# One value product of 256 columns per group, a sum moved to the branch's load, and one ring for the small tiles

## The chip, the cores and the metric

The kernel runs on one core of a Trainium2 chip. The metric is the device time of one execution in microseconds. A core has five engines that run side by side and wait for one another by semaphores: TensorE (PE, matrix products; its weight loads are listed apart as PEld), VectorE (DVE), ScalarE (ACT), GpSimd (POOL) and SyncE (SP), which here only issues DMAs. PE writes its results to PSUM, eight banks of 512 fp32 columns; the other engines read them there and put them into SBUF.

## The reference

One layer of an encoder over 1024 tokens of 1024 channels, in fp32:

```python
h = h + 0.5 * swiglu(rms_norm(h, ffn1_norm), ...)
u = rms_norm(h, mix_norm)
z = u @ w_in
q, k, v, s_in, gates = jnp.split(z, splits, axis=-1)
y_attn = neighbourhood_attention(q, k, v, na_rpb) @ w_attn_out
y_ssm = s5_branch(s_in, ...) @ w_ssm_out
g_attn, g_ssm = jnp.split(jax.nn.sigmoid(gates), 2, axis=-1)
h = h + (g_attn * y_attn + g_ssm * y_ssm) @ w_out
h = h + 0.5 * swiglu(rms_norm(h, ffn2_norm), ...)
h = h + (p @ w_ple_proj) * sigmoid(rms_norm(h, ple_norm) @ w_ple_gate)
return rms_norm(h, final_norm)
```

The attention has 8 heads of 64 channels. The tokens are a grid of 16 rows by 64 columns; each token attends to a window of 8 rows by 16 columns around it, clamped inside the grid. In the inner loop: `sc = q.k * scale + bias`, `pr = softmax(sc)`, `out = sum(pr * v)`. The other branch, S5, is a complex state-space scan over the tokens in both directions, followed by a GLU.

## The kernel before

**Two parts of every number.** The kernel gives PE its large products in fp32r, a rounded form. So that the result stays close to fp32, each operand is split into a high part, a rounded copy made on ACT, and a low part, the difference, made on DVE (`split`, L150-152). A full product is three: high x high, high x low, low x high (`mm3`, L180-184).

**Stages.** First FFN (0 to some 700 us), then the mixer (the input projections, attention, scan and GLU, to 1172 us), the two branch projections and the merge by gates, the output projection, the second FFN and the last embedding. In the mixer two streams are interleaved on PE. The main stream makes the projections: q and k of a pair of heads (`qk_proj`), and gate tiles (`gate_tile`, whose result `gs` goes to the scratch g_d in HBM). The side stream is the generator `mixer_side` (L1280 on). Each time that the main stream has issued the three products of one block it calls `tick()`, and the generator goes on after as many ticks as it asked for (4 in the first 48 units of attention, 3 after that). PE runs in exactly the order of the program; the order on DVE, ACT, POOL and SP is chosen by a planner that follows the program's priorities and a simulated time.

**Attention.** A unit is a head `hd`, a half of the rows `rb` (8 rows) and a column block `cb` of 16 columns: 8 x 2 x 4 = 64 units of 128 query tokens. A unit looks at 12 rows by 24 or 32 columns of keys, so it has 288 or 384 scores per query. Its work is spread over several steps of the loop:

- step j: `attn_scores` of unit j. Two products give the scores `s`, DVE adds the bias table, ACT makes the exponential and scales by the reciprocal of the sum; the result is `sm`.
- step j+3: `attn_turn`. Three transposes on PE into a PSUM bank `pt`; ACT copies the high part to `pth`, DVE makes the low part `ptl` (L1220, L1221).
- step j+5: `attn_values`. The weights are the values, held in `vhl` as [keys, 4 groups, 2 parts, 64 channels]. For each of three groups of keys there are two products: the values' high and low parts together (128 columns of weights) on `pth`, and the high part alone (64 columns of weights) on `ptl` (L1229, L1231). Each streams the unit's 128 queries into its 128 columns of the bank `O`, which serves four units, one (hd, rb). Channels stand on partitions 0 to 63; partitions 64 to 127 get the part of the values' low half. After the fourth unit ACT copies the upper half to `ol`, DVE adds it to the lower half, in token order, into `ot` (L1235, L1236), and ACT's queue stores `ot` to the scratch `o_d` [512, 1024].

In the loop (L1312 on) step j calls `attn_scores`, then `attn_turn`, then `attn_values`, then, for rb = 1, `load_v` of the next head (4 loads on SP, a cast on ACT, a subtraction on DVE), then two steps of the scan, which runs on POOL. From j = 48 on, each step also has `ssm_out` of one of 16 pairs of state groups: it loads two `emi` tiles on SP, copies states `xs`, and three steps later makes six products each for two groups into the bank `yo`; the result `ys` is stored to y_d. After that come the GLU's weights (`wgs`), its inputs (`yg`, split to `yh`, `yl`) and its eight products with `sg`, stored to y2_d.

**The branch's load.** `load_br(t, 0)` (L1394) loads `o_d` back for half t of the tokens, two loads of [128, 1024] into tiles `br`, and splits them; the products `br` use them at the end of the mixer.

**Rings.** A tile comes from a ring of equal slots and waits until one is free. In the mixer: the large ring `x` of 56 slots of [128, 512] (all of `tx` and `thid`: 32 slots hold u, its two parts, to the end of the mixer; `vhl`, `sm`, `pth`, `ptl`, `emi` and the GLU's split tiles share the rest); the ring of small tiles `tmp`, 4 slots (`gs`, `vf`, `row`, `ys`, `ot`, `ol`, `sg`, `wgs` and others); `st`, 3 slots of [128, 1024] (loads); `w`, 12 slots (weights and states). PSUM banks are a ring of eight.

Of the kernel before, what the change touches and what calls it, by code (L numbers as in the profile page):

```python
# [16 lines left out]
P = 128  # L17
SEQ = 1024
# [20 lines left out]
def encoder_block(ctx, tc, I, out):  # L39
# [50 lines left out]
    def dtile(name, shape):  # L90
        return dr.tile(list(shape), F32, name=name)
# [62 lines left out]
    def ksl(k):  # L154
        return slice(k * P, (k + 1) * P)
# [1057 lines left out]
    def attn_turn(cb, sm):  # L1213
        kp = 4 * KNC[cb]
        tp = bank("pt")
        for g in range(3):
            T.transpose(tp[0:kp, ksl(g)], sm[:, g * kp:(g + 1) * kp], ident)
# [6 lines left out]
    def attn_values(hd, rb, cb, O, ph, pl):  # L1224
        kp = 4 * KNC[cb]
        hl = vld[hd, cb]
        for g in range(3):

            T.matmul(O[:, ksl(cb)], lhsT=hl[0:kp, rb + g].rearrange("p h d -> p (h d)"), rhs=ph[0:kp, ksl(g)], start=(g == 0), stop=False,  # L1229
                     skip_group_check=True)  # L1230
            T.matmul(O[0:64, ksl(cb)], lhsT=hl[0:kp, rb + g, 0], rhs=pl[0:kp, ksl(g)], start=False, stop=(g == 2),  # L1231
                     skip_group_check=True)
        if cb == 3:
            ot, ol = tmp("ot"), tmp("ol")
            A.copy(ol[0:64], O[64:128])  # L1235
            V.tensor_tensor(ot[0:64].rearrange("p (r b c) -> p b r c", r=8, b=4),  # L1236
                            O[0:64].rearrange("p (b r c) -> p b r c", b=4, r=8),
                            ol[0:64].rearrange("p (b r c) -> p b r c", b=4, r=8), ALU.add)
# [41 lines left out]
    def mixer_side():  # L1280
# [31 lines left out]
        for j in range(n + 6):  # L1312
            if j < n:
                hd, rb, cb = units[j]
                while hd not in qkv:
                    yield 1
                if cb == 0 and j > 0:
                    make_tabs(hd, rb)
                sms[j] = attn_scores(hd, rb, cb)
            if 0 <= j - 3 < n:  # L1320
                pts[j - 3] = attn_turn(units[j - 3][2], sms.pop(j - 3))
            if 0 <= j - 5 < n:
                hd, rb, cb = units[j - 5]
                if cb == 0:
                    O[hd, rb] = bank("O")
                attn_values(hd, rb, cb, O[hd, rb], *pts.pop(j - 5))
                if rb == 1 and hd + 1 < NH:
                    load_v(hd + 1, cb)
            scan_steps(2)
            if j >= SO:  # L1330
                p = j - SO
# [62 lines left out]
    def load_br(t, b):  # L1394

        res = []
        if b == 0:
            for k in range(0, 4, 2):
                st = tst("br")
                nc.sync.dma_start(st.rearrange("p (k c) -> p k c", k=2),  # L1400
                                  o_d[k * P:(k + 2) * P, hsl(t)].rearrange("(k p) c -> p k c", p=P))
# [402 lines left out]
```

## Time and profile before

| | |
|---|---|
| median of 3 runs | 2105.99 us (2104.8 to 2106.98) |
| the profiled execution, its own time | 2106.49 us |
| its span | 2104.7 us |
| PE, PEld, DVE, ACT, POOL busy over the span | 99%, 81%, 67%, 48%, 19% |
| mean granted PE clock | 0.996 |
| value products on `pth` (L1229), on `ptl` (L1231) | 192 and 192, from 853 to 1109 us |
| sums of O (L1236) | 16, from 866.5 to 1113.6 us |
| PE idle in the whole span | 27.5 us |

How to read it: the time runs from launch to end on the device, the span from the first to the last instruction that the profiler shows. Durations of products overlap, because products are pipelined and their ends modelled; what a product costs is the distance from its start to the next start. "PEclk" is the part of full speed that PE's clock was granted. A row of a wait names the instruction that waited, and in brackets how long and for what.

### The profile page before, as it was taken

To read this page: it belongs to the slowest core of one execution; us is meant where nothing else is said; L and a number is where in the kernel's file an instruction comes from. 1 tells how busy PE (TensorE), PEld (TensorE's weight loads), DVE (VectorE), ACT (ScalarE), POOL (GpSimd) and SP (SyncE) were. 2 spreads that over 40 slices of the span, in tenths; PEclk is the share of its full clock that TensorE was granted. 3 is DMA by queue.
4 is the path that set the end of the run, shared out by engine and by line. 5 is a ranking of instruction groups with operands and counts; after the bars stand their busy time and mean duration, and the time that the engine had idled before them with its cause. 6 is when DMAs were issued, how large, how long until landed. Compare 5 with 4: busy or idle time off the path is not lost.

```text
span 2104.7 us, 28050 instructions
## 1 busy us (share of the span) xinstructions
PE 2077.2 (99%) x9660; PEld 1707.4 (81%) x9660; DVE 1414.2 (67%) x2420; ACT 1000.3 (48%) x1832; POOL 401.7 (19%) x636
## 2 busy tenths in 40 slices
PE   8999999999999999999999999899999999999997
PEld 3788888888888888888888888788888888888886
DVE  7897776667967334777653658896566665786855
ACT  6434333434445333667674635543333334445544
POOL 0047555541000006888100011000000000000000
PEclk9999999999999999999999999999999999999999
DMA  3434444475533552233477754143323338533302
GB/s 133 143 118 154 126 134 126 140 269 165 185 119 107 167 177 68 64 102 97 120 202 263 254 171 91 56 159 111 110 85 126 90 112 296 158 109 92 119 21 81
DMA packets 197455, 285.19 MB, mean 136 GB/s; under 512 B 41536, under 2 KB 80576, under 8 KB 197312
## 3 DMA queue, kind: packets, MB, share of 16 engines
q1 hardware_dynamic: 180160, 258.22, 38.9%
q10 hardware_dynamic: 14848, 20.98, 2.9%
q0 software_dynamic: 2304, 4.20, 1.3%
q8 instruction: 76, 1.25, 0.3%
q14 instruction: 67, 0.55, 0.1%
HBM read 201.01 MB, written 82.31 MB: 135 GB/s over the span
## 4 chain that ended last, share of the span: by engine, by line
PE 93%; DVE 4%; ACT 1%; DMA 1%; issue 1%; SPq 0%; DVEq 0%; ACTq 0%
PE dx L182 4%; PE dx L183 4%; PE dx L184 4%; PE ux L182 3%; PE ux L184 3%; PE ux L183 3%; PE gx L182 3%; PE gx L183 3%; PE gx L184 3%; PE gt L182 3%; PE gt L183 3%; PE gt L184 3%; PE dy L183 2%; PE dy L182 2%; PE dy L184 2%; PE uy L182 2%
## 5 line engine op out<-in xcount | busy, mean ns | idle before, releaser
L151 ACT CAST wh<-hbuf 128x512 fp32r<-128x512 f32 x280 | 172.9, 622 | 392.3 <-PE gx L183 84.0
L152 DVE TENSOR_TENSOR wl<-hbuf,wh 128x512 fp32r<-128x512 f32 x280 | 210.4, 754 | 125.2 <-ACT wh L151 123.0
L151 ACT CAST wh<-wblk 128x512 fp32r<-128x512 f32 x190 | 117.8, 622 | 182.5 <-PE dx L183 78.5
L182 PE MATMUL dx<-ah,wh 128*128 128x512 f32 x416 | 164.0, 394 | 3.9 <-DVE hbuf L1548 3.6
L152 DVE TENSOR_TENSOR wl<-wblk,wh 128x512 fp32r<-128x512 f32 x190 | 130.3, 688 | 53.4 <-ACT wh L151 48.0
L184 PE MATMUL dx<-ah,wl 128*128 128x512 f32 x416 | 162.3, 390 | 0.0
L183 PE MATMUL dx<-al,wh 128*128 128x512 f32 x416 | 162.3, 390 | 0.0
L152 DVE TENSOR_TENSOR al<-araw,ah 128x512 fp32r<-128x512 f32 x154 | 106.0, 692 | 53.7 <-PE dx L183 21.1
L1086 POOL TENSOR_TENSOR sc<-X,rho 128x128 f32<-128x128 f32 x128 | 77.9, 609 | 327.1 <-ACT X L1069 317.1
L182 PE MATMUL gx<-xh,wh 128*128 128x512 f32 x320 | 125.0, 391 | 1.3 <-DVE c L571 1.2
L182 PE MATMUL ux<-xh,wh 128*128 128x512 f32 x320 | 125.1, 391 | 0.3 <-DVE c L571 0.3
L184 PE MATMUL gx<-xh,wl 128*128 128x512 f32 x320 | 124.5, 389 | 0.0
L184 PE MATMUL ux<-xh,wl 128*128 128x512 f32 x320 | 124.5, 389 | 0.0
L183 PE MATMUL ux<-xl,wh 128*128 128x512 f32 x320 | 124.5, 389 | 0.0
L183 PE MATMUL gx<-xl,wh 128*128 128x512 f32 x320 | 124.5, 389 | 0.0
L151 ACT CAST ah<-araw 128x512 fp32r<-128x512 f32 x154 | 95.0, 619 | 47.5 <-PE dx L183 12.7
L182 PE MATMUL gt<-xh,wh 128*128 128x512 f32 x256 | 103.0, 402 | 0.0
L183 PE MATMUL gt<-xl,wh 128*128 128x512 f32 x256 | 99.9, 390 | 0.0
L184 PE MATMUL gt<-xh,wl 128*128 128x512 f32 x256 | 99.8, 390 | 0.0
L182 PEld LDWEIGHTS dx<-ah,wh 128*128 128x128 f32 x416 | 78.4, 188 | 21.8 <-issue 4.7
L414 DVE TENSOR_TENSOR hbuf<-hbuf 128x512 f32<-128x512 f32 x120 | 91.2, 761 | 2.1
L183 PEld LDWEIGHTS dx<-al,wh 128*128 128x128 f32 x416 | 78.5, 189 | 16.8 <-issue 0.7
(379 smaller groups left out, 5592.0 us busy)
## 6 DMA issues: line engine op xcount, KB each, us to landing
araw<-a_d SPq DMA_DIRECT2D x154, 256.0 KB
a_d<-c SPq DMA_DIRECT2D x148, 256.0 KB
wblk<-in_wd SPq DMA_DIRECT2D x88, 256.0 KB
hbuf<-in_wg SPq DMA_DIRECT2D x40, 512.0 KB
hbuf<-in_wu SPq DMA_DIRECT2D x40, 512.0 KB
wst<-in_win SPq DMA_DIRECT2D x26, 512.0 KB
hbuf<-in_xT SPq DMA_DIRECT2D x32, 256.0 KB
h_d<-hbuf ACTq DMA_DIRECT2D x32, 256.0 KB
```

The source lines that it names most:

```text
L151: A.copy(hi, src)
L152: return eng.tensor_tensor(lo, src, hi.bitcast(F32), ALU.subtract)
L182: T.matmul(o, lhsT=wh, rhs=xh, start=first, stop=False, skip_group_check=more)
L183: T.matmul(o, lhsT=wh, rhs=xl, start=False, stop=False, skip_group_check=more)
L184: T.matmul(o, lhsT=wl, rhs=xh, start=False, stop=last, skip_group_check=more)
L414: V.tensor_tensor(b11, (b12, b22, None, None, b21)[i - 2], b11, ALU.subtract)
L1086: G.tensor_tensor(sc, both, rho4, ALU.mult)
```

## The change

- `attn_turn` writes both parts of the turned weights into one tile `pb` of [keys, 3 groups, 2 parts, 128 queries], from a ring of its own with 2 slots. ACT's cast and DVE's subtraction stay, with the same sizes.
- `attn_values` makes one product per group in place of two: 128 columns of weights (both parts of the values) on 256 columns (both parts of the attention weights). A unit fills 256 columns of a bank, so a bank `O` serves two units. After every second unit ACT copies two parts (each 64 partitions x 256 columns) to the tile `O["t"]`, and DVE adds the third to the lower one. The fourth quarter, low part on low part, is not read. The upper and lower halves are no longer added here: after the fourth unit both go to `o_d`, which gets a leading dimension of 2, in one store of 128 partitions.
- `load_br(t, 0)` loads both halves (two `br` tiles per two row blocks) and DVE adds them, [128, 1024] each, before the split.
- The order in a step of the loop becomes scores, values (with `load_v`), turn.
- In the mixer the small tiles come from the large ring of 56 slots; their own ring of 4 is gone.

```diff
-    o_d = dtile("o_d", [512, SEQ])
+    o_d = dtile("o_d", [2, 512, SEQ])
...
-    cur.update(st=(ap_, "st", 3), w=(ap_, "w", 12), tmp=(ap_, "tmp", 4))
+    cur.update(st=(ap_, "st", 3), w=(ap_, "w", 12), tmp=(sb, "x", NX))
...
-        ph = thid("pth", [P, 384])
-        pl = thid("ptl", [P, 384])
-        A.copy(ph[0:kp], tp[0:kp, 0:384])
-        V.tensor_tensor(pl[0:kp], tp[0:kp, 0:384], ph[0:kp].bitcast(F32), ALU.subtract)
-        return ph, pl
+        pb = ap_.tile([P, 3, 2, P], F32R, tag="ptb", bufs=2, name="ptb")
+        src = tp[0:kp, 0:384].rearrange("p (g q) -> p g q", g=3)
+        A.copy(pb[0:kp, :, 0], src)
+        V.tensor_tensor(pb[0:kp, :, 1], src, pb[0:kp, :, 0].bitcast(F32), ALU.subtract)
+        return pb
...
+        o = O["o"][:, (cb % 2) * 256:(cb % 2) * 256 + 256]
         for g in range(3):
-            T.matmul(O[:, ksl(cb)], lhsT=hl[0:kp, rb + g].rearrange("p h d -> p (h d)"), rhs=ph[0:kp, ksl(g)], start=(g == 0), stop=False,
+            T.matmul(o, lhsT=hl[0:kp, rb + g].rearrange("p h d -> p (h d)"), rhs=pb[0:kp, g].rearrange("p h q -> p (h q)"), start=(g == 0), stop=(g == 2),
                      skip_group_check=True)
-            T.matmul(O[0:64, ksl(cb)], lhsT=hl[0:kp, rb + g, 0], rhs=pl[0:kp, ksl(g)], start=False, stop=(g == 2),
-                     skip_group_check=True)
+        if cb % 2 == 0:
+            return
+        if cb == 1:
+            O["t"] = tmp("ot")
+        ov = O["t"].rearrange("p (r b c) -> p b r c", r=8, b=4)[:, cb - 1:cb + 1]
+        src = O["o"].rearrange("p (b h r c) -> p h b r c", b=2, h=2, r=8)
+        A.copy(ov[64:128], src[64:128, 0])
+        A.copy(ov[0:64], src[0:64, 0])
+        V.tensor_tensor(ov[0:64], src[0:64, 1], ov[0:64], ALU.add)
         if cb == 3:
-            ot, ol = tmp("ot"), tmp("ol")
-            A.copy(ol[0:64], O[64:128])
-            V.tensor_tensor(ot[0:64].rearrange("p (r b c) -> p b r c", r=8, b=4),
-                            O[0:64].rearrange("p (b r c) -> p b r c", b=4, r=8),
-                            ol[0:64].rearrange("p (b r c) -> p b r c", b=4, r=8), ALU.add)
-            nc.scalar.dma_start(o_d[hd * 64:(hd + 1) * 64, hsl(rb)], ot[0:64])
+            nc.scalar.dma_start(o_d[:, hd * 64:(hd + 1) * 64, hsl(rb)], O["t"])
...
+            if 0 <= j - 5 < n:
+                hd, rb, cb = units[j - 5]
+                if cb % 2 == 0:
+                    O.setdefault((hd, rb), {})["o"] = bank("O")
+                attn_values(hd, rb, cb, O[hd, rb], pts.pop(j - 5))
+                if rb == 1 and hd + 1 < NH:
+                    load_v(hd + 1, cb)
             if 0 <= j - 3 < n:
                 pts[j - 3] = attn_turn(units[j - 3][2], sms.pop(j - 3))
-            if 0 <= j - 5 < n:
...
-                st = tst("br")
-                nc.sync.dma_start(st.rearrange("p (k c) -> p k c", k=2),
-                                  o_d[k * P:(k + 2) * P, hsl(t)].rearrange("(k p) c -> p k c", p=P))
+                st = [tst("br") for _ in range(2)]
+                for w in range(2):
+                    nc.sync.dma_start(st[w].rearrange("p (k c) -> p k c", k=2),
+                                      o_d[w, k * P:(k + 2) * P, hsl(t)].rearrange("(k p) c -> p k c", p=P))
+                V.tensor_tensor(st[0], st[0], st[1], ALU.add)
                 for i in range(2):
                     hi, lo = tx("bh"), tx("bl")
-                    split(hi, lo, st[:, hsl(i)])
+                    split(hi, lo, st[0][:, hsl(i)])
```

More of the change, by code (lines that the diff above doesn't have):

```diff
@@ L1217, in attn_turn, with attn_values @@
             T.transpose(tp[0:kp, ksl(g)], sm[:, g * kp:(g + 1) * kp], ident)
[L1218 to L1224 removed]
+        pb = ap_.tile([P, 3, 2, P], F32R, tag="ptb", bufs=2, name="ptb")
[3 more added lines that the diff above has]
+        return pb
+    def attn_values(hd, rb, cb, O, pb):
         kp = 4 * KNC[cb]
         hl = vld[hd, cb]
+        o = O["o"][:, (cb % 2) * 256:(cb % 2) * 256 + 256]
         for g in range(3):
[L1229 removed]
+            T.matmul(o, lhsT=hl[0:kp, rb + g].rearrange("p h d -> p (h d)"), rhs=pb[0:kp, g].rearrange("p h q -> p (h q)"), start=(g == 0), stop=(g == 2),
                      skip_group_check=True)
[L1231 to L1239 removed]
+        if cb % 2 == 0:
[7 more added lines that the diff above has]
+        V.tensor_tensor(ov[0:64], src[0:64, 1], ov[0:64], ALU.add)
+        if cb == 3:
+            nc.scalar.dma_start(o_d[:, hd * 64:(hd + 1) * 64, hsl(rb)], O["t"])
     ydr = y_d.rearrange("g (t o) c -> g o t c", o=16)
@@ L1319, in mixer_side @@
                 sms[j] = attn_scores(hd, rb, cb)
+            if 0 <= j - 5 < n:
[5 more added lines that the diff above has]
+                    load_v(hd + 1, cb)
             if 0 <= j - 3 < n:
                 pts[j - 3] = attn_turn(units[j - 3][2], sms.pop(j - 3))
-            if 0 <= j - 5 < n:
[L1323 to L1328, printed above, removed]
             scan_steps(2)
```

## The prediction

> **What bounds the kernel now.** I read the page first (busy shares and the chain that ended last), then the table of stretches, then TensorE's timeline through single attention units, then the waits.
>
> ```profile
> span 2104.7 us, 28050 instructions
> PE 2077.2 (99%) x9660; PEld 1707.4 (81%) x9660; DVE 1414.2 (67%) x2420; ACT 1000.3 (48%) x1832; POOL 401.7 (19%) x636
> PE 93%; DVE 4%; ACT 1%; DMA 1%; issue 1%; SPq 0%; DVEq 0%; ACTq 0%
> ```
>
> TensorE (PE) is busy 99% of the span and carries 93% of the chain. So a change counts for what it takes from PE's own stream, and for the waits that it puts into it or takes out. The next table is for the stretch that the change touches: length, busy time of PE, of weight loads (PEld), DVE, ACT and POOL, granted clock, DMA share.
>
> ```profile
> 850.00:900.00 50.00, 50.00 (x298) 43.46 (x296) 36.91 (x85) 34.32 (x76) 42.98 (x90) 1.00 0.25 74
> 1000.00:1050.00 50.00, 47.95 (x300) 42.66 (x299) 32.43 (x82) 33.80 (x78) 10.20 (x23) 0.97 0.41 118
> ```
>
> In the attention PE has no gap; DVE and ACT are at some 70%, so neither is a bound there. One stretch has a gap of 2 us and a clock under 1.
>
> **The value products.** One attention unit on PE's timeline, from its scores to the projection that follows (start, duration as modelled):
>
> ```profile
> 926.26 0.29 PE L1201 MATMUL s<-kh,qs 128*128 128x288 f32 x1
> 926.39 0.30 PE L1202 MATMUL s<-kl,qs 128*128 128x288 f32 x1
> 926.52 0.49 PE L1217 MATMUL pt<-ident,sm 128*128 128x128 f32 x3
> 926.77 0.30 PE L1229 MATMUL O<-pth,vhl 96*128 96x128 f32 x1
> ...
> 927.25 0.23 PE L1231 MATMUL O<-ptl,vhl 96*64 96x128 f32 x1
> 927.32 0.44 PE L182 MATMUL q<-xh,wh 128*128 128x512 f32 x1
> 927.60 0.40 PE L183 MATMUL q<-xl,wh 128*128 128x512 f32 x1
> ...
> 929.87 0.39 PE L184 MATMUL q<-xh,wl 128*128 128x512 f32 x1
> 930.10 0.34 PE L1201 MATMUL s<-kh,qs 128*128 128x384 f32 x1
> ...
> 931.54 0.39 PE L183 MATMUL q<-xl,wh 128*128 128x512 f32 x1
> ```
>
> Products overlap, so starts are compared, not durations. From 927.60 to 929.87 lie ten steps of 512 columns: 0.227 us each. The unit with 288 score columns runs from 926.26 to 927.60, 1.34 us, of which 0.227 is the first q product: 1.11 us for the attention part. The one with 384 columns: 931.54 - 930.10 - 0.227 = 1.21 us. What sets the pace of the six value products is seen in the weight loads of another unit:
>
> ```profile
> 922.90 0.19 PEld L1229 LDWEIGHTS O<-pth,vhl 128*128 128x128 f32 x1
> 923.01 0.14 PEld L1231 LDWEIGHTS O<-ptl,vhl 128*64 128x64 f32 x1
> 923.08 0.19 PEld L1229 LDWEIGHTS O<-pth,vhl 128*128 128x128 f32 x1
> ```
>
> They run without a gap: 0.11 us for 128 columns, 0.06 for 64, 0.17-0.18 a pair, so three pairs are 0.51-0.54 us and the next product still waits for its weights (0.28 from 927.32 to 927.60 where 0.227 is usual). The Trainium skill (TensorE: Matmul & The Clock Gate, "LDWEIGHTS (loading the stationary operand)") gives columns over 1.2 GHz, as an estimate 0.107 and 0.053 us; the rows agree within 0.02. The change keeps three loads of 128 columns and streams 256 columns behind each. The price of that is in the last stage, 24 steps between these two rows:
>
> ```profile
> 2084.74 0.28 PE L182 MATMUL pg<-xh,whh 128*128 128x256 f32 x1
> 2087.62 0.28 PE L182 MATMUL pp<-pph,whh 128*128 128x256 f32 x1
> ```
>
> 2.88 / 24 = 0.12 us for 256 columns with a new load each. A unit in the new order is then 0.13 + 0.13 (scores) + 3 x 0.12 (values) + 3 x 0.11 (transposes, a load of 128 columns each) = 0.95 us, against 1.11. With 384 columns: 0.18 + 0.18 + 0.36 + 0.33 = 1.05 against 1.21. That is 0.16 us in both, times 64 units = 10.2 us off PE. Bounds: 0.13 if the load behind the transposes still shows by 0.03 (8.3 us), 0.20 if the whole of 0.54 - 0.36 and a bit of the late projection comes back (12.8 us).
>
> **The place where PE waited.** The small tiles leave a ring of 4 for the ring of 56. What the 4 cost is in this place:
>
> ```profile
> 1033.39 4.06 DMA y_d<-ys
> 1037.53 0.56 DVE L1180 TENSOR_TENSOR row<-bt,rowm 128x384 f32<-128x384 f32 x1 [2.66 <-DMA y_d<-ys]
> 1040.87 0.68 DVE L1236 TENSOR_TENSOR ot<-O,ol 64x512 f32<-64x512 f32 x1
> 1034.73 0.23 PE L1231 MATMUL O<-ptl,vhl 96*64 96x128 f32 x1
> 1036.41 0.40 PE L183 MATMUL gt<-xl,wh 128*128 128x512 f32 x1
> 1039.33 0.22 PE L1231 MATMUL O<-ptl,vhl 96*64 96x128 f32 x1
> 1041.60 0.79 PE L1111 MATMUL yo<-emi 128*128 128x128 f32 x2 [2.05 <-DVE ot L1236]
> 1044.75 0.46 PE L183 MATMUL gt<-xl,wh 128*128 128x512 f32 x1
> ```
>
> `row` (L1180) and `ys` are both small tiles. DVE stood 2.66 us for a slot that a store of `ys` still held; `ot` behind it came late, and PE stood 2.05 us for it. After that PE ran slower for a while. From the last value product to the second projection product it took 5.42 us here and 1.68 in the unit before, so 3.74 us were lost. With 24 slots beside the 32 that hold u, `row` need not wait for that store: I take 3.7 us off. Bounds: 0 if another wait takes its place, 4.3 if the 0.54 us wait quoted under the rivals goes too.
>
> **Evacuation.**
>
> ```profile
> L1235 ACT COPY ol<-O 64x512 f32<-64x512 f32 x15 | 8.8, 584 | 1.8 <-DMA y_d<-ys 1.4
> L1115 ACT COPY ys<-yo 128x256 f32<-128x256 f32 x16 | 5.9, 367 | 2.9 <-PE yo L1113 1.7 <-DMA y_d<-ys 0.9
> L1236 DVE TENSOR_TENSOR ot<-O,ol 64x512 f32<-64x512 f32 x15 | 10.2, 680 | 4.2 <-ACT ol L1235 4.1
> L1165 DVE TENSOR_TENSOR vhl<-vf,vhl 128x256 fp32r<-128x256 f32 x14 | 6.9, 491 | 5.1 <-ACT vhl L1164 5.1
> L152 DVE TENSOR_TENSOR wl<-wst,wh 128x1024 fp32r<-128x1024 f32 x14 | 18.4, 1316 | 2.4 <-PE s L1201 1.6 <-PE yo L1113 0.7
> ```
>
> Per head and half ACT makes four copies of 256 columns out of PSUM in place of one of 512 at 0.58: by the nearest row 0.37 each, together +0.9 us (at most 0.58 each, +1.75). DVE makes two sums of about 0.49 in place of one of 0.68: +0.3. Over the four units, some 15.5 us, ACT goes from about 10.6 busy to 11.6 of 14.9 us, 78%; DVE stays below that. Nothing of this is on PE's path as long as an O bank comes back before PE runs round the eight; O is now held for two units rather than four. If the cover is gone, the 16 x 0.9 = 14 us that ACT gains in work (28 at most) are what it could cost. The splits of the weights cost the same as before; their pair has two slots, and values now run ahead of the transposes, so the slot is free when the next pair is written. `load_v` moves with the values: four loads on SP, a cast on ACT and a subtraction on DVE per block now stand ahead of the transposes' cast and subtraction, whose reader is two units off; no queue entry of SP or POOL lies between the old place and the new. Stores of O stay 16 issues on ACT's queue, of 256 KB for 128.
>
> **The branch's load.** Eight loads in place of four go through a ring of three, and four sums of 128x1024 are added on DVE, 1.32 us each by L152. When are they due?
>
> ```profile
> 1146.36 2.67 SPq L1400 DMA_DIRECT2D br<-o_d  x2
> 1143.05 2.56 ACT L151 CAST bh<-br 128x512 fp32r<-128x512 f32 x4
> L182 PE MATMUL br<-bh,wh x32: 389/389/389, 1172.2 to 1193.3; 128*128 128x512 f32 x32
> 1173.56 1.29 DVE L152 TENSOR_TENSOR bl<-br,bh 128x512 fp32r<-128x512 f32 x2 [1.07 <-ACT bh L151]
> ```
>
> The first half is split from 1143 and used from 1172: 29 us of cover. The second is split until 1174.9 and due 24 products later, at 1172.2 + 24 x 0.227 = 1177.6: 2.7 us of cover. Its loads were issued from 1146 on, 27 us before the split of 1173.56, so the sums fit ahead of the splits; if they don't, up to 2 x 1.32 us of sum plus a late fourth load show, less the 2.7. On SP a fourth load that waits for a slot holds the g_d stores and h_d loads behind it; in a ring of 56 the stores' tiles are not missed at once. I take 0; bounds 0 and +4.
>
> **Sum.** The profiled execution took 2106.49 us (span 2104.7, 1.8 around it), 0.5 above the median of 2105.99. 2106.5 - 10.2 - 3.7 = 2092.6; I add 1.1 for two waits of the 0.54 kind in the crowded last units: 2093.7, in terms of the median about 2093.
>
> **Rivals.** *Given back in part.* The big ring is crowded in units 48 to 63.
>
> ```profile
> 1090.27 0.46 PE L1111 MATMUL yo<-emi 128*128 128x128 f32 x2 [0.54 <-DMA emi<-u_d]
> 1086.95 3.19 DMA emi<-u_d
> SPq L1096 <- PE yo L1113: 1.0, 3, 0.4
> ```
>
> SP already waits there for slots that state products (yo) set free, and PE once for a load that came late. Counting tiles from the code: 32 of u, 4 to 8 of values, 4 of softmax, 8 of emi are up to 52 of 56; the pairs (6) leave, and some 5 to 9 small tiles come. If the 3.7 us wait merely moves, or a few of 1 us appear, the time is 2097 to 2101.
>
> *Slower: the full ring starves the state products.* If small tiles take the slots early and each of the 16 pairs' emi loads is issued only when a slot frees, PE waits at every pair, for between 0.54 (the one seen) and 3.19 us (the whole landing). At 1.5 us that is +24: 2117. It decides from 14 / 16 = 0.87 us per pair. For it: the count above. Against: in most pairs emi is issued several microseconds ahead, and total room (60 slots of both rings, then 56 and the pairs outside) is not less.
>
> *No gain in the products.* If columns streamed set the pace, 6 x 128 and 3 x 256 cost the same 0.36 us (3 x 0.12), and only the wait's 3.7 us remain: 2102. The gapless loads and the 0.51 us of the six speak against it. The Trainium skill (TensorE: Matmul & The Clock Gate, "Back-to-back issue gap") has a gap formula for isolated products, by which I estimate 0.335 us for the six and 0.328 for the three; this trace disagrees with it for the six (0.51). The same section says that in a stream of loads and products both set the spacing, and with that the rows agree.
>
> *It does not do what it says.* DVE, ACT and SP are ordered by a planner; a new order can put waits of a few microseconds anywhere behind the attention and leave nothing measurable.
>
> **Chances.** A measurement can tell about 0.2% (4.2 us) from no change: 2101.8 to 2110.2. Forecast (2087 to 2097) 0.60; given back in part 0.24; no gain in the products 0.02; planner 0.05; starved ring 0.09. So faster 0.84, same 0.07, slower 0.09. Low end: 2106 - 12.8 - 4.3 = 2089, and 3 us for an order that happens to be better; high end 2104, which leaves out the starved ring and part of the planner's case.
>
> **What the profile after would show.** Right: O products 3 per unit, 256 columns, 0.12 us apart; the part from scores to projection 0.95 and 1.05 us; no DVE wait of `row` for a `ys` store and clock 1.00 in all stretches of the attention; ACT near 78% there. Wrong if: starts of O are over 0.15 us apart; yo waits for emi at many pairs; ACT waits for slots of `gs` or `sg` around the GLU, where 32 of u, 8 of its weights and 16 of its inputs fill all 56; or the first products of branch 0's second half wait for a sum.

## The result, and the profile after

The changed kernel takes 2179.15 us (median of 4 runs, 2171.54 to 2182.62) against 2106.48 for the kernel before on the same chip: a ratio of 1.034 (95% interval 1.0328 to 1.0353). The forecast was 2093. The profiled execution took 2177.57 us, 71.1 more than the one of before; the spans differ by 71.0. The page of the changed kernel, busy times and chain:

```profile
span 2175.7 us, 27724 instructions
PE 2098.3 (96%) x9468; PEld 1711.9 (79%) x9468; DVE 1417.7 (65%) x2440; ACT 1011.0 (46%) x1882; POOL 400.9 (18%) x636
PE 78%; DMA 9%; DVE 6%; ACT 4%; SPq 2%; issue 1%; DVEq 0%; ACTq 0%
```

PE is still busy nearly always, but its share of the chain fell from 93 to 78%, and transfers hold 9% of it. No engine got much more work (ACT 11 us, DVE 4). PE now waits. The two stretches shown of before, in the changed kernel (length, then PE, PEld, DVE, ACT, POOL busy, granted clock, DMA share, GB/s):

```profile
850.00:900.00 50.00, 50.00 (x261) 43.03 (x260) 33.07 (x85) 33.93 (x83) 42.79 (x93) 1.00 0.23 69
1000.00:1050.00 50.00, 43.96 (x221) 37.60 (x222) 34.86 (x90) 36.74 (x89) 17.90 (x39) 0.93 0.27 85
```

At 850 the attention runs without a gap; at 1000 PE stands 6 of 50 us and its clock falls. One unit on PE's timeline, as the change makes it:

```profile
888.61 0.29 PE L1201 MATMUL s<-kh,qs 128*128 128x288 f32 x1
888.74 0.30 PE L1202 MATMUL s<-kl,qs 128*128 128x288 f32 x1
888.87 0.52 PE L1231 MATMUL O<-ptb,vhl 96*128 96x256 f32 x3
889.23 0.49 PE L1217 MATMUL pt<-ident,sm 128*128 128x128 f32 x3
889.48 0.48 PE L182 MATMUL k<-xh,wh 128*128 128x512 f32 x1
889.79 0.39 PE L183 MATMUL k<-xl,wh 128*128 128x512 f32 x1
```

Three value products start 0.36 us ahead of the transposes, so 0.12 each, and the attention part is 889.79 - 888.61 - 0.227 = 0.95 us. That is the forecast to the hundredth, so the loss lies elsewhere. The waits of PE between 680 and 1340 us (who waited for whom: us in total, times, longest):

```profile
PE br L182 <- ACT bh L151: 13.3, 3, 6.0
PE pt L1217 <- ACT gs L1362: 10.5, 4, 5.1
PE yo L1111 <- DVE ptb L1221: 4.6, 4, 1.2
```

They name ACT and DVE, which are busy for 66 to 73% of the two stretches above: those wait in their turn. The chain through 905 to 960 us (start, us) and ACT's waits for the loads of v, of the changed kernel and then of the kernel before:

```profile
910.03 7.52 DMA vf<-v_d
926.71 8.19 DMA vf<-v_d
945.27 8.74 DMA o_d<-ot
956.29 2.29 DMA vf<-v_d
```

```profile
  DMA vf<-v_d: 64.2, 22
```

```profile
  DMA vf<-v_d: 13.3, 10
```

A load of v that is free takes 2.3 us, others take 7.5 to 8.6, and on the whole chain of the attention the store of O itself takes 8.7 to 11.1. The DMA view of the changed kernel from 1014 to 1024 us, with one such store in it (busy share of the 16 DMA engines in 40 slices, GB/s, and the share of ACT's queue):

```profile
DMA  3221211222123012111111111111111111111000
GB/s 69 57 59 28 68 38 28 47 56 55 38 57 46 0 53 50 53 56 57 41 57 49 52 43 55 46 46 47 54 46 47 46 54 47 45 35 30 2 0 0
q10 hardware_dynamic: 130, 0.26, 7.9%
```

While hardly anything but the 256 KB of this store is under way, the busy share stays at 1 tenth and the rate at 41 to 57 GB/s. A stretch in the store that ends the chain's row of 945.27, with the share in hundredths (last columns: clock, DMA share, GB/s):

```profile
951.00:953.00 2.00, 2.00 (x14) 1.79 (x14) 1.74 (x4) 1.66 (x4) 1.64 (x5) 1.00 0.13 48
```

0.13 is two engines of sixteen. The store's target has two planes, and its outermost dimension is 2. The Trainium skill (DMA: Bandwidth & Descriptors, "Why a DMA increments its semaphore by 16 and not by 1") states that a DMA runs on the largest number of engines up to 16 that divides the outermost dimension of both sides; the trace agrees, with 2.

To see where the 71 us lie I cut each profile at the first start of a group of PE's products and at their last (us; "state products" from the first yo to the last, "branch" from the first br of L182 to the last br). The stretches are those of the profiled execution, the time is the median of the runs:

| kernel | time | sin to scores | scores to first yo | state products | branch | rest |
|---|---|---|---|---|---|---|
| before | 2106.5 | 151.1 | 193.8 | 73.4 | 86.8 | 1599.6 |
| after | 2179.2 | 162.1 | 205.9 | 99.5 | 107.5 | 1600.7 |
| e1 two stores | 2138.2 | 162.2 | 187.7 | 78.9 | 107.3 | 1600.5 |
| e3 only the ring | 2141.9 | 161.1 | 196.4 | 79.9 | 102.9 | 1600.3 |
| e5 only the order | 2110.8 | 152.1 | 194.1 | 78.3 | 86.8 | 1599.9 |
| e9 before, rings 11/3 | 2105.0 | 151.6 | 193.8 | 73.1 | 86.8 | 1597.8 |
| e7 two stores, rings 11/3 | 2112.3 | 152.1 | 187.5 | 76.2 | 94.6 | 1599.9 |
| e12 one store, rings 11/3 | 2185.1 | 152.4 | 225.9 | 100.7 | 96.4 | 1609.3 |
| e8 sums at evacuation, 11/3 | 2105.6 | 151.8 | 187.5 | 75.9 | 86.8 | 1599.0 |
| e14 the same, 10/5 | 2093.2 | 152.6 | 187.5 | 68.4 | 86.8 | 1596.0 |
| e16 two stores, 10/5 | 2101.1 | 151.4 | 187.5 | 71.0 | 87.1 | 1600.7 |
| e17 before, 10/5 | 2104.3 | 151.5 | 193.8 | 70.1 | 86.8 | 1601.7 |
| e22 e14 with 8 stores into planes | 2108.5 | 151.2 | 188.9 | 81.8 | 86.8 | 1596.4 |
| e23 e14 with 8 flat stores | 2094.9 | 151.8 | 187.6 | 69.2 | 86.8 | 1596.6 |
| e24 one flat store, 10/5 | 2103.5 | 151.2 | 187.5 | 67.5 | 96.0 | 1600.4 |
| e25 e14 in the large ring | 2127.7 | 160.7 | 187.5 | 72.7 | 104.4 | 1602.5 |

"11/3" means 11 weight tiles and 3 small tiles in rings of their own. The rest is the stretch before sin, the pieces between, and some 845 us behind the branch. From kernel to kernel it moves by some 3 us either way (in e12 it is 9.7 more than before, nearly all between the last state product and the GLU), so a single difference of 3 us isn't read as an effect.

### The profile page after: what moved, and what is told of

Read it like the earlier page. It is cut to its first block, busy times and chain, and to the rows that moved or that the text cites. A ratio compares the mean times of both kernels' runs of the same rounds, so it can differ in the third digit from the quotient of the medians.

```text
span 2175.7 us, 27724 instructions
## 1 busy us (share of the span) xinstructions
PE 2098.3 (96%) x9468; PEld 1711.9 (79%) x9468; DVE 1417.7 (65%) x2440; ACT 1011.0 (46%) x1882; POOL 400.9 (18%) x636
## 4 chain that ended last, share of the span: by engine, by line
PE 78%; DMA 9%; DVE 6%; ACT 4%; SPq 2%; issue 1%; DVEq 0%; ACTq 0%
PE dx L182 4%; PE dx L183 4%; PE dx L184 4%; PE gx L182 3%; PE ux L182 3%; PE gx L184 3%; PE ux L184 3%; PE ux L183 3%; PE gx L183 3%; DMA o_d<-ot 3%; DMA vf<-v_d 2%; PE dy L183 2%; PE dy L182 2%; PE dy L184 2%; PE gy L182 2%; PE uy L182 2%
## 5 line engine op out<-in xcount | busy, mean ns | idle before, releaser
L182 PE MATMUL dx<-ah,wh 128*128 128x512 f32 x416 | 164.3, 395 | 1.4 <-DVE hbuf L1555 1.1
L182 PE MATMUL gx<-xh,wh 128*128 128x512 f32 x320 | 125.0, 390 | 1.2 <-DVE c L571 1.2
L182 PE MATMUL ux<-xh,wh 128*128 128x512 f32 x320 | 125.0, 390 | 0.0
L182 PE MATMUL gt<-xh,wh 128*128 128x512 f32 x256 | 104.8, 410 | 2.8 <-ACT ys L1115 2.8
L182 PEld LDWEIGHTS dx<-ah,wh 128*128 128x128 f32 x416 | 78.4, 189 | 19.5 <-DVE hbuf L1555 1.9
```

The source lines that it names most:

```text
L182: T.matmul(o, lhsT=wh, rhs=xh, start=first, stop=False, skip_group_check=more)
```

## The experiments

**The change with one part undone, and two parts alone.** Two stores of 64 partitions in place of one of 128:

```diff
-            nc.scalar.dma_start(o_d[:, hd * 64:(hd + 1) * 64, hsl(rb)], O["t"])
+            for w in range(2):
+                nc.scalar.dma_start(o_d[w, hd * 64:(hd + 1) * 64, hsl(rb)], O["t"][w * 64:(w + 1) * 64])
```

> The changed kernel with each 128-partition store of O made as two stores of 64 partitions each; nothing else. Theory S (slow store): the store to the two halves of o_d runs on two of the sixteen DMA engines (DMA share 0.13, 46 to 48 GB/s, 8 to 9 us), and the slots and value loads behind it starve PE; with two stores of the old form it lands in under 4 us and most of the 46 us lost in the attention units come back: 2125 to 2140. Theory R (ring): the small tiles in the ring of 56 starve the planner's order by themselves: 2165 to 2182, PE still waits in the units.

Measured: 2138.16 us, ratio 1.015 (1.0133 to 1.0168). That is within theory S. The same bytes in twice as many issues are 41 us faster than the change. The stretch from the scores to the first state product falls from 205.9 to 187.7 us, below the 193.8 of before. 32 us of loss remain, nearly all from sin to the scores and in the branch.

The kernel before with the small tiles in the large ring, and nothing else of the change:

```diff
-    cur.update(st=(ap_, "st", 3), w=(ap_, "w", 12), tmp=(ap_, "tmp", 4))
+    cur.update(st=(ap_, "st", 3), w=(ap_, "w", 12), tmp=(sb, "x", NX))
```

> The kernel before with only the small tiles put into the large ring. Theory S: only the losses outside the units appear, 10 us before the first scores and some around the GLU: 2112 to 2135, no new loss per unit. Theory R: the units lose as well, 2150 or more. My forecast of a gain from the removed wait of row for ys: 2102.

Measured: 2141.86 us, ratio 1.0175 (1.016 to 1.019). That is above theory S, whose range ended at 2135, and below theory R. The shared ring alone costs 36 us: 10.0 from sin to the scores, 16.1 in the branch, and 9.1 in the attention, where theory S expected no new loss. What it does in the first of these is seen on DVE, where the blocks of the projections' input are normalised (xn, a small tile) and split. Kernel before:

```profile
698.96 2.74 DVE L254 SCALAR_TENSOR_TENSOR xn<-hbuf,gains,rs 128x512 f32<-128x512 f32 x4
702.75 2.49 DVE L152 TENSOR_TENSOR xl<-xn,xh 128x512 fp32r<-128x512 f32 x4
```

Changed kernel:

```profile
707.84 0.69 DVE L152 TENSOR_TENSOR xl<-xn,xh 128x512 fp32r<-128x512 f32 x1 [0.69 <-ACT xh L151]
708.44 0.75 DVE L254 SCALAR_TENSOR_TENSOR xn<-hbuf,gains,rs 128x512 f32<-128x512 f32 x1
709.88 0.69 DVE L152 TENSOR_TENSOR xl<-xn,xh 128x512 fp32r<-128x512 f32 x1 [0.69 <-ACT xh L151]
```

Before, four xn are made in a row, and ACT casts one while DVE makes the next. After, the next xn starts only when the xl of the last is through, DVE stands 0.69 us for ACT in each block, and a block takes 709.88 - 707.84 = 2.04 us in place of (2.74 + 2.49) / 4 = 1.3. This run (e3) has the same pattern, with xl at 707.97 and 710.01. PE's own waits for these blocks are only 1.8 us in e3, but its granted clock falls to 0.50 between 715 and 720 us, and from 710 to 720 us it starts 20 products where the kernel before starts 48. In effect the small tiles have one slot there, not four; as I read it, u and the prefetches fill the large ring, and a small tile gets a place only as its predecessor leaves. That it is the ring is shown by this run, whose only edit it is; how the ring comes to have one slot for them is not shown.

The kernel before with the values ahead of the transposes, and nothing else of the change:

```diff
-            if 0 <= j - 3 < n:
-                pts[j - 3] = attn_turn(units[j - 3][2], sms.pop(j - 3))
             if 0 <= j - 5 < n:
                 hd, rb, cb = units[j - 5]
...
                 if rb == 1 and hd + 1 < NH:
                     load_v(hd + 1, cb)
+            if 0 <= j - 3 < n:
+                pts[j - 3] = attn_turn(units[j - 3][2], sms.pop(j - 3))
```

> The kernel before with only the order changed, values ahead of the turn. Both theories: within 0.2% of 2106; if the order itself cost, 2110 or more.

Measured: 2110.79 us, ratio 1.0027 (1.0015 to 1.0039). PE's waits for the parts of the weights are new:

```profile
PE O L1229 <- ACT pth L1220: 3.0, 3, 1.9
PE O L1231 <- DVE ptl L1221: 2.5, 4, 1.6
```

A value product now stands one turn of transposes nearer to the cast that it needs. These 5.5 us are about the measured loss of 5.0. So the order by itself costs something. With the joint product and rings of 10/5 (e14, e16, e24) no such wait is left; in the changed kernel PE still waits for `ptb` (1.9 us in O, 3.4 in pt, 4.6 in yo). No run has the joint product without the new order.

Then two stores, with the small tiles in a ring of 3 of their own and 11 weight tiles:

```diff
-    cur.update(st=(ap_, "st", 3), w=(ap_, "w", 12), tmp=(sb, "x", NX))
+    cur.update(st=(ap_, "st", 3), w=(ap_, "w", 11), tmp=(ap_, "tmp", 3))
```

> The changed kernel with two stores and with the small tiles in a ring of their own, of 3 slots, paid for with one slot of the ring w (11 in place of 12). Theories S and R together: both losses gone, the product gain of 10 us stays, less what 3 slots for 4 cost: 2094 to 2106. If neither store nor ring is the cause: over 2150.

Measured: 2112.29 us, ratio 1.003 (1.002 to 1.0039). That is 6 us above the range expected. With store and ring undone, the loss from sin to the scores is gone (152.1); the branch still takes 94.6 us against 86.8, and the product's gain shows only up to the first state product.

**Sums and rings.** To take the branch's load out of the question the two halves are summed where they are evacuated, and store and load are those of before (rings 11/3):

```diff
-        A.copy(ov[64:128], src[64:128, 0])
-        A.copy(ov[0:64], src[0:64, 0])
+        A.copy(ov[0:64], src[64:128, 0])
+        V.tensor_tensor(ov[0:64], src[0:64, 0], ov[0:64], ALU.add)
         V.tensor_tensor(ov[0:64], src[0:64, 1], ov[0:64], ALU.add)
```

> The 256-column value products stay, but the two halves are summed where they are evacuated: one ACT copy and two DVE additions for two units, one store of 64 rows into an O buffer without the leading 2, and the branch's load without sums, as in the kernel before. Small tiles in their own ring of 3, weights in a ring of 11. Theory A (the products are worth 0.12 us a unit, and the 8 us that the variant with two stores and the ring of 3 lost in the branch come from the sums in the branch's load): the stretch from first score to first state product stays near 187.5 us, the stretch of the branch's first products to their last goes back from 94.6 to 86.8, and the time is 2098 to 2103, ratio 0.996 to 0.999. Rival B (the 8 us come from the rings of 11 and 3, whose shortage is felt around the GLU): the branch's stretch stays near 94 and the time is 2106 to 2112. Rival C (two DVE additions for two units are too much on DVE, which then holds the state products): waits of yo or O for ot appear, and the stretch of state products grows beyond 80 us.

Measured: 2105.56 us, ratio 0.9997 (0.9988 to 1.0006). The branch is back at 86.8, as theory A has it, but the time is 3 us above its range: the state products take 75.9 us.

The same with 10 weight tiles and 5 small tiles:

> As the variant that sums at the evacuation, with 10 weight tiles for 11 and 5 small tiles for 3, in the same memory. Theory A (small tiles wait for slots that stores hold, weights come early enough): 1 to 5 us below the variant with 11 and 3, 2094 to 2101. Rival B (a ring of 10 is short for the weights, whose loads then wait): above it by 2 us or more, and PE waits for weights (w or wh) in the projections.

Measured: 2093.2 us, ratio 0.9941 (0.9929 to 0.9953). This beats both kernels. Theory A has the sign but not the size: the time is 12.4 us below the variant with 11/3, where it gave 1 to 5, and just under its 2094. The state products fall from 75.9 to 68.4 us, the rest by 3.0. The waits of PE between 680 and 1300 us that are left:

```profile
PE pt L1217 <- ACT sm L1210: 1.4, 1, 1.4
PE v L1392 <- DVE wl L152: 0.8, 1, 0.8
PE v L1391 <- ACT wh L151: 0.5, 1, 0.5
```

Two controls change only the rings of the kernel before, to 11/3 and to 10/5:

> The kernel before with nothing changed but the rings: 11 weight tiles for 12 and 3 small tiles for 4, as the variants with a ring of 3 have them. Theory A: the rings of 11 and 3 cost next to nothing (2105 to 2109, ratio 0.9995 to 1.0015; the branch's stretch stays near 86.8 us). Rival B: they are what costs 8 us in the branch's stretch (2112 to 2116, ratio 1.003 to 1.005).

> The kernel before with nothing changed but the rings: 10 weight tiles and 5 small tiles for 12 and 4. Theory A (of the 12 us that the variant with sums at the evacuation gained, 6 to 8 are the products, 4 to 6 the small tiles, since the place where PE waited 2.05 us for ot and ran slower behind it is gone): 2099 to 2102, no wait of yo for ot. Rival B (the small tiles matter only together with the new order of the values): 2104 to 2107, and the wait for ot stays. Rival C (the rings are the whole gain): 2093 to 2095.

Measured: 2104.95 us, ratio 0.9995 (0.9986 to 1.0003), and 2104.34, ratio 0.9995 (0.9986 to 1.0004). Neither moves the time, and rings of 11/3 leave the branch at 86.8 us. So the 12 us of the variant with sums at the evacuation are not a gain of the rings alone. With 10/5 the wait of yo for ot is gone, as theory A said, and the state products take 70.1 us for 73.4; but the rest takes 2.1 us more, so the time is 2 us above theory A's range and in rival B's.

Two stores and the sums in the branch's load, with 10/5:

> The change with each store of O as two of 64 rows, the sums in the branch's load as the change has them, and rings of 10 weight tiles and 5 small tiles. Against the variant that sums at the evacuation with the same rings (2093.2) only the place of the sums differs. Theory A (the sums in the branch's load cost 8 us, since they stand on DVE ahead of the GLU's last products): 2099 to 2104, and the stretch of the branch's first products to their last is 93 to 97 us against 86.8. Rival B (with 5 small tiles the GLU's stores come back early enough and the sums hide): 2091 to 2095, stretch 87 to 89. Rival C (the doubled stores and loads cost as well): above 2105.

Measured: 2101.08 us, ratio 0.9978 (0.9969 to 0.9987). The time is in theory A's range but its reason isn't there: the branch takes 87.1 us, as rival B had it. Of the 6.4 us by which its span is over that of e14, 2.6 are in the state products (three waits for emi, 2.1 in all) and 4.7 in the rest, 3.8 of these behind the branch. What orders those I did not settle.

**The slow store by itself.** One store into two planes, with the rings of e7:

> The changed kernel with its single store of 128 rows into two planes, but with small tiles in their own ring of 3 and weights in a ring of 11. It completes the square of store (one, two) by ring (shared, own): 2179 (one, shared), 2138 (two, shared), 2112 (two, own). Theory A (the slow store does its harm in any ring, since the tile that it holds is one of few): the difference of one store to two stays near 40 us or grows, 2145 to 2165, with waits of ACT and DVE for o_d<-ot in the stretch from first score to last state product. Rival B (the slow store hurts only where it holds a slot that everything else needs, the shared ring): the difference falls below 12 us, 2112 to 2124.

Measured: 2185.07 us, ratio 1.0372 (1.0356 to 1.0388), 73 us above e7, and beyond theory A's range. So the store does its harm in any ring, and more in the small one. Who waited for it there (tile view of ot):

```profile
  DVE row L1180: 18.6, 2
  ACT gs L1362: 15.2, 2
```

That is one way: the tile that it holds. The other, as I read it, is that the loads of v have a part of their bytes on the same two engines. To part them, a further store that nobody reads was put behind the stores of e14, from a tile that stays anyway, once into two planes and once into rows that follow one another:

```diff
+    n_d = dtile("n_d", [2, 512, SEQ])
...
+            nc.scalar.dma_start(n_d[:, hd * 64:(hd + 1) * 64, hsl(rb)], u[0][0][0].bitcast(F32))
```

(flat: `n_d` of `[8, P, SEQ]`, and `n_d[hd, :, hsl(rb)]` as the target)

> The variant with sums at the evacuation and rings of 10 and 5 (2093.2), and behind each of its 16 stores of O a further store on ACT's queue that nobody reads: 128 partitions of a resident tile into two planes, the shape of the change's store. It holds no slot that anybody waits for. Theory A (the slow store does harm by what else has to go over the two DMA engines that it fills, the loads of v above all): 2120 to 2160, loads of v for which ACT waits 7 to 8 us. Rival B (it does harm only by the slot of the small tile that it holds): 2093 to 2099.

> As the variant with the further store into two planes, but the same 128 partitions and 256 KB go to rows that follow one another (the leading dimension is 128, not 2). Theory A (what is slow is the leading 2, and not the bytes or the 16 further issues): 2093 to 2097, and each of the further stores lands in 2 to 4 us, on all 16 engines. Rival B (256 KB more per store are too much beside the other traffic): the same as the variant with two planes, within 10 us.

Measured: 2151.36 us, ratio 1.022 (1.0206 to 1.0234), and 2094.66, ratio 0.9949 (0.9936 to 0.9963). As a test of the two ways it missed: the planner drew all 16 further stores ahead of the attention, to 646 us and later, since their source was there already. As a test of the shape it is plain. GB/s in 40 slices and ACT's queue, two planes from 690 to 700 us and flat from 646 to 662:

```profile
GB/s 49 49 49 57 49 49 49 57 49 49 49 49 57 49 49 57 49 49 49 49 57 49 49 57 49 49 49 49 57 49 49 123 98 229 401 311 66 49 66 369
q10 hardware_dynamic: 294, 0.59, 15.3%
```

```profile
GB/s 143 358 77 379 374 389 297 220 189 307 410 405 405 410 400 394 333 364 410 410 405 410 405 410 410 405 405 405 399 410 394 405 399 282 215 261 405 405 400 394
q10 hardware_dynamic: 2565, 4.69, 80.9%
```

49 GB/s against 400 for the same tile and the same 256 KB; of the 5.72 MB moved in the flat stretch 4.69 are ACT's queue. With the flat stores the time is 1.5 us above e14's, and the intervals of the two overlap. The slow ones filled the way of everything behind them, and PE began on sin 58 us later (743.2 against 685.0).

Eight such stores with a source that depends on the loads of v, so that they stay in the attention:

```diff
+            if rb == 0:
+                nc.scalar.dma_start(n_d[:, hd * 64:(hd + 1) * 64], vld[hd, 2].rearrange("p a h d -> p (a h d)").bitcast(F32))
```

> The variant with sums at the evacuation and rings of 10 and 5 (2093.2), and behind every second store of O one store that nobody reads, of a tile of values that is needed for some 11 us more anyway: 128 partitions into two planes. Its source depends on the loads of v, so it cannot be issued ahead of the attention. Theory A (the harm is done by what else has to go over the two DMA engines that the store fills, the loads of v above all): 8 stores, half of the change's 16, which cost 73 us beside a ring of 3: +20 to +45, 2113 to 2138, and ACT waits 7 to 8 us for single loads of v. Rival B (the harm is done by the slot of the small tile that the store holds): +0 to +5, 2093 to 2098.

> The same 8 further stores, 128 rows one after the other in the target (leading dimension 128). Both theories: 2093 to 2097; above 2100 the further issues on ACT's queue or the bytes themselves would be a cost that the comparison with two planes must leave out.

Measured: 2108.47 us, ratio 1.0016 (1.0007 to 1.0025), and 2094.85, ratio 0.995 (0.9936 to 0.9963). Eight stores into planes that hold no small tile themselves cost 13.6 us, below theory A's range and above rival B's; 12.6 us of it lie in the state products. The chain of the run with two planes, 840 to 1170 us:

```profile
912.02 10.24 DMA o_d<-ot
922.28 0.70 DVE row L1181
1036.44 10.02 DMA n_d<-vhl
1080.13 8.96 DMA vf<-v_d
```

The kernel's own store of 128 KB, quick in its own layout, takes 10.24 us beside the slow one, and a load of v 8.96. So the engines' share comes back as held tiles: `row` starts only when that quick store has landed, and in all `row` waits 8.0 us for tiles ot in this run. Doubled, for 16 stores, 13.6 us are some 27 of the 73 us, as an estimate; e12 also has 3 small tiles where e22 has 5. How the 73 us divide between the engines and the held tiles stays open.

**The change mended, and the ring once more.** O's buffer as rows of a head that follow one another, rings of 10/5, all else as the change has it:

```diff
-    o_d = dtile("o_d", [2, 512, SEQ])
+    o_d = dtile("o_d", [8, P, SEQ])
...
-            nc.scalar.dma_start(o_d[:, hd * 64:(hd + 1) * 64, hsl(rb)], O["t"])
+            nc.scalar.dma_start(o_d[hd, :, hsl(rb)], O["t"])
...
+                    for i in range(2):
+                        nc.sync.dma_start(st[w][i * 64:(i + 1) * 64].rearrange("p (k c) -> p k c", k=2),
+                                          o_d[2 * k:2 * k + 4, w * 64:(w + 1) * 64, hsl(t)].rearrange("(k i) p c -> i p k c", i=2)[i])
```

> The change as it stands, one store of 128 rows and the sums in the branch's load, but O's buffer is laid out so that the 128 rows of a head follow one another (leading dimension 128), and small tiles have a ring of 5 of their own, weights 10. The branch's load takes four loads of 64 partitions a pair in place of two of 128. Theory A (the shape of the store and the shared ring are all that was wrong with the change): 2093 to 2101, as the variant with two stores and the same rings (2101.1) or a little below. Rival B (one store of 256 KB per head and half is too much in any shape, or the smaller loads are late for the sums): above 2105, with waits of DVE for br<-o_d.

Measured: 2103.51 us, ratio 0.9992 (0.9983 to 1.0001): between the two ranges, and no gain over the kernel before. Up to the end of the state products it is the quickest of all (67.5 us for those); then the branch takes 96.0 us. The waits of DVE for br<-o_d that rival B named are there, 20.8 us in four, against 6.5 in three in e16. The four smaller loads a pair are thus a second difference from e16 beside the store, and this run does not part them. Here one sees what the sums in the load do. DVE, ACT and PE of this run:

```profile
1150.41 1.22 DVE L1409 TENSOR_TENSOR br<-br 128x1024 f32<-128x1024 f32 x1 [3.31 <-DMA br<-o_d]
1157.49 1.23 DVE L1409 TENSOR_TENSOR br<-br 128x1024 f32<-128x1024 f32 x1 [5.26 <-DMA br<-o_d]
1158.63 0.69 DVE L1280 TENSOR_TENSOR sg<-sg,yg 128x512 f32<-128x512 f32 x1
```

```profile
1152.69 0.69 ACT L1279 ACTIVATE sg<-glu,glub 128x512 f32<-128x512 f32 x1 [5.33 <-DVE sg L1280]
```

```profile
1170.20 0.80 PE L182 MATMUL br<-bh,wh 128*128 128x512 f32 x1 [5.29 <-ACT bh L151]
```

DVE stands 3.31 us for the load of one sum, and the GLU's product sg (L1280) behind it holds up ACT's next sg by 5.33 us. Then DVE stands 5.26 us for the load of the next sum, and again an sg starts only behind it. The GLU's stores and the branch's next loads wait for that, ACT's casts bh stand behind those loads, and PE stands 5.29 us. Then it runs at half clock for a while (PE, PEld, DVE, ACT, POOL busy, clock, DMA):

```profile
1165.00:1170.00 5.00, 0.00 (x0) 0.00 (x0) 3.03 (x4) 3.81 (x5) 0.00 (x0) 1.00 0.61 153
1170.00:1175.00 5.00, 4.42 (x10) 3.14 (x11) 4.62 (x7) 4.30 (x7) 0.00 (x0) 0.51 1.10 252
1175.00:1180.00 5.00, 5.00 (x19) 4.04 (x18) 4.19 (x6) 4.54 (x6) 0.00 (x0) 0.80 1.05 340
```

5.3 us of waiting became 9.2 us of branch. The Trainium skill (TensorE: Matmul & The Clock Gate, "Part 1: The HAM clock gate (the "warmup" mystery)") puts the clock at half after at least one idle window of about 3.4 us, until after at least one busy window of that length. The rows agree: half after 5.29 us of idling, and until 1177, some 6.8 us from PE's next start (0.80 over five us is half speed for two of them). The wait of 5.3, half of 6.8 and a further wait of 0.4 are 9.1 of the 9.2 us.

The small tiles of e14 in the large ring:

> The variant with sums at the evacuation, whose store and branch load are as in the kernel before, with small tiles in the large ring and 12 weight tiles, as the change has them. Theory A (the shared ring costs by itself what it cost alone in the kernel before, 36 us, and what it cost beside two stores, 37): 2125 to 2135, +10 from the first sin to the first score, the rest around the GLU and the branch. Rival B (it costs only beside other slow steps; with the freed tiles of the softmax weights it is roomy): 2093 to 2105.

Measured: 2127.7 us, ratio 1.0104 (1.009 to 1.0118), 34.5 above e14 and in theory A's range. 8.1 us are lost from sin to the scores and 17.6 in the branch, where PE's waits are

```profile
PE br L182 <- ACT bh L151: 10.6, 4, 6.3
```

without any sum in the branch's load. So the ring costs by itself what it cost in two other settings: 36 (e3), 37 (e1 against e16), 34.5; in the last two the weight tiles differ too, 12 against 10.

## Why the prediction was wrong, step by step

**The step that failed first** is "Stores of O stay 16 issues on ACT's queue, of 256 KB for 128". I counted issues and bytes and gave them no price. The term put at nothing was the landing: 8.7 to 11.1 us on two engines. After less e1 it is 41 us in the shared ring, e12 less e7 it is 73 in a small one. Nothing of it was in the range.

**The second** is "With 24 slots beside the 32 that hold u, `row` need not wait for that store". I took the ring for roomy in the units where I had seen a wait, and did not count it where the tiles are many: at the projections' input and around the GLU and the branch. That total room "is not less" counted slots and not how long each is held. Priced at -3.7, it measures +34.5 to +37. The rival with a starved ring had the right sign, but its place was wrong: the state products wait for emi once, 1.0 us. The place named last, under "Wrong if" (the GLU, where u, weights and inputs fill all 56), is nearer to where the branch lost 16 to 18 us.

**The third** is the branch's load, "I take 0; bounds 0 and +4". I asked when the sums' results are due and found 2.7 us of cover. I did not ask who is queued behind a sum that waits: the GLU's sg on DVE. With small tiles in a ring of their own it costs 0.3 us (e16), 7.8 (e7) and 9.2 (e24) in the branch's stretch. DVE's wait in the last sum goes with it, 2.12, 4.86 and 5.26 us, and so does PE's wait for bh, none, 4.0 and 5.3; why the last load comes later in one than in the other I did not settle. The upper bound of 4 was too low, since it left out the half clock that follows a long wait of PE. In the change's own ring the sums add little: the branch takes 107.3 us with them (e1) and 104.4 without (e25), 2.9 more, which is within the bounds. So in the changed kernel this step did little of the harm in the branch.

**Right: the value products.** 0.95 us for the small unit, and from 928.52 to 929.79 in e14, less 0.227, 1.04 for the large one. The whole gain is less than 0.16 a unit, for the projection steps became a little longer. In e14 ten of them lie between these rows:

```profile
926.00 0.39 PE L183 MATMUL q<-xl,wh 128*128 128x512 f32 x1
...
928.29 0.39 PE L184 MATMUL q<-xh,wl 128*128 128x512 f32 x1
928.52 0.34 PE L1201 MATMUL s<-kh,qs 128*128 128x384 f32 x1
...
929.79 0.39 PE L183 MATMUL q<-xl,wh 128*128 128x512 f32 x1
```

That is 0.229 each in place of 0.227, at a granted clock of 1.00 in both. By the starts of the scores between 880 and 1000 us, a unit takes 3.75 us against 3.89 before. The table's stretches of e14 against e17, which has the same rings, give 6.3 + 1.7 = 8.0 us, just under the lower bound of 8.3. The 6.3 stand firm: the stretch is 193.8 us in before, e9 and e17 and 187.5 in e7, e8, e14, e16 and e24. The other 4.6 us by which the spans of e14 and e17 differ lie elsewhere, 5.7 less in the rest and 1.1 more from sin to the scores, and the product does not explain them. The rival of no gain falls.

**Right in size, but not by the change: the place where PE waited.** The state products get shorter by 73.4 - 70.1 = 3.3 us with 5 small tiles in their own ring (3.7 forecast). In the large ring other waits took its place.

**Evacuation.** The groups in the changed kernel (duration min, median, max in ns):

```profile
L1240 ACT COPY ot<-O x32: 367/368/373, 867.0 to 1163.6; 64x256 f32<-64x256 f32 x32
L1242 DVE TENSOR_TENSOR ot<-O,ot x32: 406/416/419, 867.8 to 1164.4; 64x256 f32<-64x256 f32 x32
```

Four copies of 0.367 for one of 0.584 are +0.88 per head and half, as forecast (+0.9); two sums of 0.416 for one of 0.680 are +0.15 (forecast +0.3). PE has no wait for a slot of O. ACT is 68% busy from 850 to 900, below the forecast 78. The move of the values, taken at nothing, is the one doubtful term here: alone it costs 5 us (e5), and in e14 no wait of it is seen.

**The sum as runs give it:** product and rings 10/5 with sums at the evacuation -12.1 (e14), sums moved to the branch's load and two stores +7.9 (e16), shared ring +37.1 (e1), one store into two planes +41.0 (after): 73.9, where 72.7 were measured. Each part is the step from one run to the next, so they add up by construction, and the sum is an account and no proof. That e14 lands at the forecast's 2093 is luck and no merit of the sum: its store, ring and load are not those that were priced, and a part of its gain lies in stretches that the forecast did not touch.

## What to carry to other kernels

Price a store by what it holds until it lands, and look at the outermost dimension of both its sides: a new leading 2 can cost more than the bytes. Before tiles move into a shared ring, find the stretch in which the ring is fullest over the whole life of the kernel, not the one where the edit lies. Where an instruction is put on an in-order engine with a load as its input, the price is read from what stands behind it there.

## What the runs showed of the hardware that was not expected

- A store of 256 KB from 128 partitions into two planes moved at 49 GB/s; into 128 rows that follow one another at about 400, some other traffic included (e20, e21). Beside such a store a load of v rose from 2.3 to between 7 and 9 us, and a store of 128 KB to 10.24 (e22).
- ACT's queue paid as well: the issue of a store took 0.50 us into two planes, 0.45 from 64 partitions and 0.33 flat (medians, after, before and e24); with slow stores in a row the median issue was 4.9 us (e20).
- The projections' pace of 0.227 us a product went to 0.229 with the joint value products, at an unchanged granted clock. What sets it is open.
